# Layer norm with GELU on one core: the first row tile loaded in 32 and 96 partitions, the second from ScalarE's queue

## Chip, cores, metric

One core of a Trainium2 chip. The metric is device time in microseconds (us) of one execution. Before: 320.3 us, median of 6 runs (319.95 to 320.45). A profile's span is some 1.8 us shorter than the time of the same run.

## The reference

```python
x: (8, 1024, 2048) float32; gamma, beta: (2048,)
normalized = (x - mean(x, -1)) / sqrt(var(x, -1) + eps)
out = gamma * normalized + beta
return 0.5 * out * (1 + tanh(sqrt(2 / pi) * (out + 0.044715 * out ** 3)))
```

67.1 MB are read and 67.1 MB are written.

## The kernel before

The 8192 rows are 16 blocks of 4 MB, each of four row tiles (128 partitions x 2048). Five slots hold one block each; the result overwrites the input in its slot, is stored from there, and only then may the slot be loaded again.

```python
xg = xf.rearrange("(b p r) d -> b p r d", p=P, r=R)      # R = 4, SLOTS = 5, SPLIT = 3
# SyncE: all loads
for b in range(B):
    s = slot(b)
    if stored(b):
        sy.wait_ge(s_store[s], stored(b))
    for q in range(R):
        if b == 0:
            sy.dma_start(out=xts[s][:, q:q + 1], in_=xg[0, :, q:q + 1]).then_inc(s_first[q], 16)
        elif b == SPLIT:
            sy.dma_start(out=xts[s][:, q:q + 1], in_=xg[b, :, q:q + 1]).then_inc(s_load[s], 16)
    if b not in (0, SPLIT):
        sy.dma_start(out=xts[s], in_=xg[b]).then_inc(s_load[s], 16 * R)
# ScalarE: parameters, then arithmetic and stores
ac.preload_act_table(ACT.Gelu_apprx_tanh)
for k, (p, src) in enumerate(((64, gamma), (0, beta), (32, beta))):
    ac.dma_start(out=row(p), in_=src.rearrange("(o k f) -> o k f", o=1, k=K)).then_inc(s_par[k], 16)
... # [cut: beta to bf16, g_t from PSUM, then per tile yk = (x - mean) * rstd and the GELU; a store per block,
    #       in the last block one per tile]
# VectorE
for q in range(R):
    stats(slot(0), q, (s_first[q], 16), q + 1)
    ...  # [cut: after tile 0 it waits for g_t = gamma on all partitions, which eight matmuls make from gamma's row]
```

Of the kernel before, what the change touches and what calls it, by code (L numbers as in the profile page):

```python
# [10 lines left out]
R = 4  # L11
SLOTS = 5
SPLIT = 3
K = 16


@with_exitstack
def kernel(
# [9 lines left out]
    P = 128  # L28
# [9 lines left out]
    xg = xf.rearrange("(b p r) d -> b p r d", p=P, r=R)  # L38
# [8 lines left out]
    def sb(name, shape, dt):  # L47
        return pool.tile(shape, dt, name=name)

    xts = [sb(f"xt{s}", [P, R, d], f32) for s in range(SLOTS)]  # L50
    yks = [sb(f"yk{s}", [P, d], bf16) for s in range(2)]
    zgs = [sb(f"zg{s}", [P, d], bf16) for s in range(2)]
    pss = [psum.tile([P, d], f32, name=f"ps{s}") for s in range(2)]
    rows = sb("rows", [65, K, d // K + 4], f32)
    ones = sb("ones", [65, P], f32)
# [12 lines left out]
    def sem(name):  # L68
        return tc.alloc_semaphore(name)

    s_first = [sem(f"first{q}") for q in range(R)]
# [17 lines left out]
    def slot(b):  # L89
        return (b + SLOTS - 1) % SLOTS  # L90

    def row(p):
        return rows[p:p + 1, :, :d // K]

    def split(v):
        return v.rearrange("o (k f) -> o k f", k=K)

    def cols(j):
        return slice(j * FMAX, (j + 1) * FMAX)

    def by_row(b):
        return b == B - 1

    def stored(b):
        return sum(16 * (R if by_row(c) else 1) for c in range(b) if slot(c) == slot(b))

    with tc.tile_critical(no_gpsimd_drain=True):  # L107
        with nc.Block(no_gpsimd_drain=True) as block:

            @block.sync  # L110
            def _(sy):
                for b in range(B):
                    s = slot(b)
                    if stored(b):
                        sy.wait_ge(s_store[s], stored(b))
                    for q in range(R):
                        if b == 0:
                            sy.dma_start(out=xts[s][:, q:q + 1], in_=xg[0, :, q:q + 1]).then_inc(s_first[q], 16)
                        elif b == SPLIT:
                            sy.dma_start(out=xts[s][:, q:q + 1], in_=xg[b, :, q:q + 1]).then_inc(s_load[s], 16)  # L120
                    if b not in (0, SPLIT):
                        sy.dma_start(out=xts[s], in_=xg[b]).then_inc(s_load[s], 16 * R)
# [21 lines left out]
            @block.vector  # L144
            def _(ve):
                def stats(s, q, wait, count):
                    xr = xts[s][:, q].rearrange("p (s f) -> p s f", f=FMAX)
                    for j in range(nsub):
                        ins = ve.bn_stats(out=sts[:, q, j, :], in_=xr[:, j, :])  # L149
                        if j == 0 and wait:  # L150
                            ins._wait_ge(*wait)
                            if wait[0] is s_load[s]:
                                ins.then_inc(s_load[s], -16 * R)
                    ins.then_inc(s_o, 1)
                    ve.bn_aggr(out=mvs[:, q], in_=sts[:, q])._wait_ge(s_o, count).then_inc(s_a, 1)  # L155

                def scale(q, count):
                    ve.tensor_tensor(out=zgs[q % 2], in0=yks[q % 2], in1=g_t,  # L158
                                     op=ALU.mult)._wait_ge(s_n, count).then_inc(s_z, 1)

                ve.memset(b_hl, 0.0).then_inc(s_m, 1)  # L161
                for q in range(R):
                    stats(slot(0), q, (s_first[q], 16), q + 1)
                    if q == 0:

                        ve.tensor_tensor(out=split(b_hl[32:33]), in0=row(32), in1=split(b_hl[32:33]),  # L166
                                         op=ALU.subtract)._wait_ge(s_c, 2).then_inc(s_m, 1)
                        ve.wait_ge(s_c, 3)
                    else:
                        scale(q - 1, q)  # L170
                ve.sem_inc(s_o, -R)
                ve.sem_inc(s_n, -(R - 1))
                with ve.Fori(0, (B - 1) // SLOTS):
                    for k in range(SLOTS * R):
                        s, q = divmod(k, R)
                        stats(s, q, (s_load[s], 16 * R) if q == 0 else None, k + 1)
                        scale((q - 1) % R, k + 1)
                    ve.sem_inc(s_o, -SLOTS * R)
                    ve.sem_inc(s_n, -SLOTS * R)
                scale(R - 1, 1)  # L180

            @block.scalar
            def _(ac):
                ac.preload_act_table(ACT.Gelu_apprx_tanh)  # L184
                for k, (p, src) in enumerate(((64, gamma), (0, beta), (32, beta))):
                    ac.dma_start(out=row(p), in_=src.rearrange("(o k f) -> o k f", o=1, k=K)).then_inc(s_par[k], 16)
                ac.wait_ge(s_m, 1)
                ac.activation(out=split(b_hl[0:1]), in_=row(0), func=ACT.Identity)._wait_ge(s_par[1], 16).then_inc(s_c, 1)  # L188
                ac.activation(out=split(b_hl[32:33]), in_=row(32),  # L189
                              func=ACT.Identity)._wait_ge(s_par[2], 16).then_inc(s_c, 1)  # L190
                ac.activation(out=g_t, in_=pss[0], func=ACT.Identity)._wait_ge(s_tg, 1).then_inc(s_c, 1)  # L191
                for t in range(T + 1):
                    if t < T:
                        b, q = divmod(t, R)
                        ac.activation(out=yks[t % 2], in_=xts[slot(b)][:, q], func=ACT.Identity, scale=rss[:, q:q + 1],  # L195
                                      bias=nms[:, q:q + 1])._wait_ge(s_p, t + 1).then_inc(s_n, 1)
                    i = t - 1
                    if i < 0:
                        continue
                    b, q = divmod(i, R)  # L200
                    xt = xts[slot(b)]
                    ins = ac.activation(out=xt[:, q], in_=pss[i % 2], func=ACT.Gelu_apprx_tanh)._wait_ge(s_t, i + 1)  # L202
                    if by_row(b):
                        ins.then_inc(s_r, 1)
                        ac.dma_start(out=og[b, :, q:q + 1], in_=xt[:, q:q + 1])._wait_ge(  # L205
                            s_r, b + q + 1).then_inc(s_store[slot(b)], 16)
                        ac.sem_inc(s_g, 1)
                    elif q == R - 1:
                        ins.then_inc(s_r, 1)
                        ac.dma_start(out=og[b], in_=xt)._wait_ge(s_r, b + 1).then_inc(s_store[slot(b)], 16)  # L210
                        ac.sem_inc(s_g, 1)
                    else:
                        ins.then_inc(s_g, 1)

            @block.tensor
            def _(pe):

                pe.wait_ge(s_setp, 2)
                for j in range(nsub):
                    ins = pe.matmul(pss[0][:, cols(j)], lhsT=ones[64:65],  # L220
                                    rhs=rows[64:65, j * K // nsub:(j + 1) * K // nsub, :d // K], start=True, stop=True)
                    if j == 0:
# [60 lines left out]
```

## Time and profile before

| | before |
|---|---|
| time | 320.3 us |
| span of the profiled run | 318.5 us |
| bytes moved, at 430 GB/s | 134.24 MB, 312 us |
| gamma lands, g_t is ready | 6.02, 15.17 us |
| first store issued | 36.02 us |
| last load has landed for its user | 285.0 us |
| last store issued | 310.32 us |

The prediction shows the slices, the chain and the start. To read them: transfers are the bound from 3 us to 314 us (the DMA digit is 9 from the second slice to the last but one), so ask of every change what it does to the bytes moved by a given moment.

### The profile page before, as it was taken

Reading aid. Unit: us, or ns where it says so; the run is one execution under the profiler, and the core shown is the slowest. Engines: PE = TensorE matmul, PEld = TensorE weight load, DVE = VectorE, ACT = ScalarE, POOL = GpSimd, SP = SyncE. Lnnn points to the kernel's source line nnn. Section 1 sums busy time; section 2 is a strip of 40 time slices with the busy share of each in tenths; the row PEclk is TensorE's granted clock in tenths of the full one; section 3 lists DMA queues with packets and bytes.
Section 4 is the critical chain, followed back from the end, with each engine's and each line's share of the span. In section 5 each row is a group of like instructions: output and inputs, shape, how many; then the busy total and the mean of one; then the engine's idle time right before and its main releaser. Section 6 shows DMA issues by size and latency. Waiting matters only on the chain.

```text
span 318.5 us, 2090 instructions
## 1 busy us (share of the span) xinstructions
PE 244.3 (77%) x520; PEld 57.2 (18%) x520; DVE 247.5 (78%) x386; ACT 251.7 (79%) x132; POOL 110.6 (35%) x201
## 2 busy tenths in 40 slices
PE   2769999999999989687795868958589595886860
PEld 1212222222212112111121112212112121111110
DVE  3499999999999897786968968599686986869810
ACT  2769999999999989698696967969589695995970
POOL 1144444444444444232443333333332433324300
DMA  7999999999999999999999999999999999999995
GB/s 289 438 457 401 394 434 430 444 424 436 432 424 444 417 453 416 440 440 416 457 403 457 420 436 444 411 461 403 453 432 424 449 407 457 424 432 403 453 396 209
DMA packets 6002, 134.26 MB, mean 421 GB/s; under 512 B 704, under 2 KB 752, under 8 KB 752
## 3 DMA queue, kind: packets, MB, share of 16 engines
q1 hardware_dynamic: 3168, 67.11, 49.4%
q10 hardware_dynamic: 2832, 67.13, 49.0%
q14 instruction: 2, 0.02, 0.0%
HBM read 67.13 MB, written 67.11 MB: 421 GB/s over the span
## 4 chain that ended last, share of the span: by engine, by line
DMA 64%; ACT 14%; DVE 10%; POOL 5%; PE 3%; issue 1%; ACTq 0%; DVEq 0%; POOLq 0%; SPq 0%
DMA xt<-in_x_dram 32%; DMA out_dram<-xt 30%; ACT yk L195 9%; DVE sts L149 7%; ACT xt L202 4%; POOL ves L135 3%; DVE zg L158 2%; PE ps L220 2%; DMA rows<-in_gamma_dram 2%; POOL rss L137 2%; POOL nms L139 1%; DVE mvs L155 1%; PE ps L237 1%; ACT g_t L191 1%; ACTq L205 0%
## 5 line engine op out<-in xcount | busy, mean ns | idle before, releaser
L149 DVE BATCH_NORM_STATS2 sts<-xt 128x6 f32<-128x512 f32 x256 | 157.7, 679 | 33.5 <-DMA xt<-in_x_dram 31.9
L195 ACT ACTIVATE yk<-xt,nms,rss 128x2048 bf16<-128x2048 f32 x64 | 133.7, 2090 | 48.9 <-POOL nms L139 42.9
L237 PE MATMUL ps<-zg,ident 128*128 128x512 bf16 x256 | 120.8, 627 | 55.8 <-DVE zg L158 54.7
L233 PE MATMUL ps<-b_hl,ones_b 33*128 33x512 bf16 x256 | 120.6, 624 | 2.2 <-PEq L228 2.2
L202 ACT ACTIVATE xt<-ps 128x2048 f32<-128x2048 f32 x64 | 118.9, 1858 | 1.5 <-PE ps L237 1.5
L135 POOL TENSOR_SCALAR ves<-mvs 128x1 f32<-128x1 f32 x64 | 38.5, 602 | 179.2 <-DVE mvs L155 179.2
L158 DVE TENSOR_TENSOR zg<-yk,g_t 128x2048 bf16<-128x2048 bf16 x64 | 76.5, 1195 | 19.2 <-ACT yk L195 19.2
L237 PEld LDWEIGHTS ps<-zg,ident 128*128 128x128 bf16 x256 | 27.6, 130 | 149.0 <-DVE zg L158 113.7
L233 PEld LDWEIGHTS ps<-b_hl,ones_b 33*128 33x128 bf16 x256 | 27.0, 127 | 92.1 <-issue 88.4
L139 POOL TENSOR_SCALAR nms<-mvs,rss 128x1 f32<-128x1 f32 x64 | 35.7, 558 | 6.3
L137 POOL TENSOR_TENSOR rss<-ves,mhalf 128x1 f32<-128x1 f32 x64 | 35.3, 552 | 5.3
L155 DVE BATCH_NORM_AGGREGATE mvs<-sts 128x2 f32<-128x24 f32 x64 | 16.9, 264 | 2.2
L220 PE MATMUL ps<-rows,ones 1*128 1x512 f32 x8 | 7.2, 1076 | 6.1 <-DMA rows<-in_gamma_dram 6.1
L188 ACT ACTIVATE b_hl<-rows 1x2048 bf16<-1x2048 f32 x1 | 1.9, 1909 | 5.3 <-DMA rows<-in_beta_dram 5.3
L166 DVE TENSOR_TENSOR b_hl<-rows,b_hl 1x2048 bf16<-1x2048 f32 x1 | 2.3, 2280 | 2.8 <-ACT b_hl L189 2.8
L220 PEld LDWEIGHTS ps<-rows,ones 1*128 1x128 f32 x8 | 2.5, 327 | 9.2 <-DMA rows<-in_gamma_dram 6.1
L191 ACT ACTIVATE g_t<-ps 128x2048 bf16<-128x2048 f32 x1 | 1.9, 1877 | 1.9 <-PE ps L220 1.9
L184 ACT ACT_TABLE_LOAD x1 | 1.3, 1283 | 0.9 <-SPq L107 0.9
L189 ACT ACTIVATE b_hl<-rows 1x2048 bf16<-1x2048 f32 x1 | 1.9, 1908 | 0.0
L161 DVE MEMSET b_hl<- 33x1024 uint32 x1 | 0.9, 912 | 1.2 <-SPq L107 1.2
L126 POOL MEMSET ones<- 65x128 f32 x1 | 0.2, 202 | 0.5 <-SPq L107 0.5
L130 POOL TENSOR_SCALAR_AFFINE_SELECT ident<-ident 128x128 bf16<-128x128 bf16 x1 | 0.3, 295 | 0.1
(7 smaller groups left out, 0.9 us busy)
## 6 DMA issues: line engine op xcount, KB each, us to landing
out_dram<-xt ACTq DMA_DIRECT2D x15, 4096.0 KB, 32.6
xt<-in_x_dram SPq DMA_DIRECT2D x14, 4096.0 KB
xt<-in_x_dram SPq DMA_DIRECT2D x8, 1024.0 KB, 8.4
out_dram<-xt ACTq DMA_DIRECT2D x4, 1024.0 KB, 8.6
rows<-in_beta_dram ACTq DMA_DIRECT2D x2, 8.0 KB, 5.9
rows<-in_gamma_dram ACTq DMA_DIRECT2D x1, 8.0 KB, 5.1
```

Source lines behind the costliest of these rows:

```text
L135: po.tensor_scalar(out=ves[:, c], in0=mvs[:, k, 1:2], scalar1=float(eps), scalar2=1.0, op0=ALU.add, op1=ALU.mult)._wait_ge(s_a, k + 1).the ...
L137: po.tensor_tensor(out=rss[:, c], in0=ves[:, c], in1=mhalf, op=ALU.pow)._wait_ge(s_q, 2 * k + 1).then_inc(s_q, 1)
L139: po.tensor_scalar(out=nms[:, c], in0=mvs[:, k, 0:1], scalar1=rss[:, c], scalar2=-1.0, op0=ALU.mult, op1=ALU.mult)._wait_ge(s_q, 2 * k + 2 ...
L149: ins = ve.bn_stats(out=sts[:, q, j, :], in_=xr[:, j, :])
L155: ve.bn_aggr(out=mvs[:, q], in_=sts[:, q])._wait_ge(s_o, count).then_inc(s_a, 1)
L158: ve.tensor_tensor(out=zgs[q % 2], in0=yks[q % 2], in1=g_t, op=ALU.mult)._wait_ge(s_n, count).then_inc(s_z, 1)
L191: ac.activation(out=g_t, in_=pss[0], func=ACT.Identity)._wait_ge(s_tg, 1).then_inc(s_c, 1)
L195: ac.activation(out=yks[t % 2], in_=xts[slot(b)][:, q], func=ACT.Identity, scale=rss[:, q:q + 1], bias=nms[:, q:q + 1])._wait_ge(s_p, t + ...
L202: ins = ac.activation(out=xt[:, q], in_=pss[i % 2], func=ACT.Gelu_apprx_tanh)._wait_ge(s_t, i + 1)
L220: ins = pe.matmul(pss[0][:, cols(j)], lhsT=ones[64:65], rhs=rows[64:65, j * K // nsub:(j + 1) * K // nsub, :d // K], start=True, stop=True)
L233: ins = pe.matmul(ps[:, cols(j)], lhsT=ones_b, rhs=b_hl[:, cols(j)], start=True, stop=False)
L237: ins = pe.matmul(ps[:, cols(j)], lhsT=ident, rhs=zgs[k % 2][:, cols(j)], start=False, stop=True)
```

## The change

The intent is to start the stream of loads earlier: a small first load (32 partitions) should be issued faster, and a second queue should feed the engines from the start.

```diff
+FEW = 32
 ...
-                        if b == 0:
+                        if b == 0 and q == 0:
+                            for p in (slice(0, FEW), slice(FEW, P)):
+                                sy.dma_start(out=xts[s][p, q:q + 1], in_=xg[0, p, q:q + 1]).then_inc(s_first[q], 16)
+                        elif b == 0 and q != 1:
                             sy.dma_start(out=xts[s][:, q:q + 1], in_=xg[0, :, q:q + 1]).then_inc(s_first[q], 16)
 ...
-                    stats(slot(0), q, (s_first[q], 16), q + 1)
+                    stats(slot(0), q, (s_first[q], 32 if q == 0 else 16), q + 1)
 ...
             def _(ac):
+                ac.dma_start(out=xts[slot(0)][:, 1:2], in_=xg[0, :, 1:2]).then_inc(s_first[1], 16)
                 ac.preload_act_table(ACT.Gelu_apprx_tanh)
```

## The prediction

The sum: 320.22 - 0.5 + 0 = 319.7 us. In step 3, that tiles 0 and 1, 2 MB, pass ahead of gamma is the assumption.

> **What bounds the kernel now.** I read the 40 slices first, then the chain that ended last, then the first 20 us and the last 35 us in order of time with the bytes moved in each. The program has 64 tiles of 128 rows in 16 blocks of 4 MB; five buffers of one block each; loads on SyncE's queue, stores and the three parameter loads on ScalarE's.
>
> The slices: the DMA line is at 9 from the second to the last but one, while no compute engine is above 79% of the span.
>
> ```profile
> PE 244.3 (77%) x520; PEld 57.2 (18%) x520; DVE 247.5 (78%) x386; ACT 251.7 (79%) x132; POOL 110.6 (35%) x201
> DMA  7999999999999999999999999999999999999995
> GB/s 289 438 457 401 394 434 430 444 424 436 432 424 444 417 453 416 440 440 416 457 403 457 420 436 444 411 461 403 453 432 424 449 407 457 424 432 403 453 396 209
> HBM read 67.13 MB, written 67.11 MB: 421 GB/s over the span
> ```
>
> 134.24 MB have to pass. At the level of the middle slices (about 430 GB/s) that is 312 us; the span is 318.5. So some 6.5 us are not transfer at full rate: a start before the pipe is full, and an end. The change works on the start.
>
> The chain (start us, us, what): compute in the beginning, later store landing to load to landing, then the last block's arithmetic.
>
> ```profile
> 0.92 5.09 DMA rows<-in_gamma_dram
> 6.06 7.21 PE ps L220 x8
> 13.29 1.89 ACT g_t L191
> 15.27 2.48 DVE sts L149 x4
> ...
> 68.79 26.55 DMA out_dram<-xt
> 95.35 33.54 DMA xt<-in_x_dram
> ...
> 250.80 34.20 DMA xt<-in_x_dram
> ```
>
> It names gamma as the first link, since row tile 1 waits for the gamma product (15.27). This is where one can be misled: the chain follows who released whom, but the 26.55 and 33.54 us are transfers lying in a full queue. Store landings at 95.33 (block 2) and 250.79 (block 10) are 8 blocks apart: 19.43 us a block, 216 GB/s, half of 430. From the first store (issued at 36.0) stores and loads thus share the pipe in halves, and stores are never short of work: 36.0 + 0.34 + 3 x 19.43 = 94.6, against 95.33 seen. What sets the end is bytes over rate, plus when the pipe began to be full.
>
> The beginning, in stretches of 0.2 us (last columns DMA share and GB/s):
>
> ```profile
> 1.60:1.80 0.20, 0.00 (x0) 0.00 (x0) 0.20 (x1) 0.20 (x1) 0.20 (x1) 1.00 0.00 0
> 1.80:2.00 0.20, 0.00 (x0) 0.00 (x0) 0.20 (x1) 0.20 (x1) 0.02 (x1) 1.00 0.62 123
> 2.20:2.40 0.20, 0.00 (x0) 0.00 (x0) 0.00 (x0) 0.00 (x0) 0.00 (x0) 1.00 1.22 205
> 2.80:3.00 0.20, 0.00 (x0) 0.00 (x0) 0.00 (x0) 0.00 (x0) 0.00 (x0) 1.00 0.33 123
> 3.00:3.20 0.20, 0.00 (x0) 0.00 (x0) 0.00 (x0) 0.00 (x0) 0.00 (x0) 1.00 1.36 573
> ```
>
> SyncE begins its first load at 0.93; nothing moves before 1.8; from 1.8 to 3.0 it is some 170 GB/s, and full after 3.0. By 4.0 us 0.65 MB have moved, as much as a pipe at 430 GB/s would move in 1.51 us: the effective start is 4.0 - 1.51 = 2.5 us. That number is what the change can lower.
>
> [...] halves of 216 GB/s each when both queues are full. So no bandwidth is to be had here, only issue time. [...] here it is 0.87 us (0.93 to 1.80) for the 128-partition load, and its issue on SyncE took 0.775 us, the later ones of this line 0.376 to 0.43. [...]
>
> **The change part by part.**
>
> 1. Row tile 0 in 32 + 96 partitions. One issue more on SyncE (about 0.4 us by the later ones), and tile 1's is gone from it: the same count of four. [...] How much of its 0.775 us is a fixed cost the trace doesn't say; my estimate is that the first byte comes 0.1 to 0.4 us earlier, at 1.4 to 1.7.
>
> 2. Tile 1 on ScalarE's queue. It is issued there at 0.92, beside SyncE's first, not after it (before, SyncE's second load began near 1.7). From about 1.8 two queues feed the engines. The gap between 1.8 and 3.0, 0.2 MB moved where 0.52 would fit at 430, is worth (0.52 - 0.2)/0.43 = 0.7 us if filled entirely. But at 2.0 to 2.4 the share is already above 1 at only 205 to 246 GB/s, so a part is the first packets' own latency, which stays. I take a third to a half: 0.2 to 0.35 us.
> Sum of 1 and 2: effective start earlier by 0.3 to 0.75 us, the middle near 0.5.
>
> 3. Gamma and both betas behind tile 1 in the same queue. [...] 2 MB: 4.9 us at 430, so near 6.7 to 7 us; landing 1 to 2 us after that (tile 0's bytes were through near 5.0 and its consumer began at 5.86). Gamma then lands at 8 to 9 instead of 6.02: 2 to 3 us later. Tile 0, sharing the pipe with tile 1, lands near 7 to 7.5 instead of 5.83. Gamma is the later, and 7.2 us of matmuls and the 1.89 us copy follow it. So VectorE's second statistics start at 17.3 to 18.3 instead of 15.27, and all arithmetic and the first store (36.0) are 2 to 3 us later.
>
> 4. What this delay costs. While no store is there, loads take the whole pipe, so it isn't idle. Up to 36.3 some 0.43 x (36.3 - 2.5) = 14.5 MB are loaded of the 21 MB that five buffers admit; then 216 GB/s up to the first store's landing near 55.8 give 4.2 MB more, so about 2.3 MB of loads are in hand when the next is allowed. Three us of delay take 3 x 0.216 = 0.65 MB of these. They do not run out. Later VectorE waits for loads anyhow (31.9 us in 11 times), so arithmetic catches up. Cost at the end: 0.
>
> 5. The table preload starts some 0.6 us later behind the added issue; it was done at 2.17 and its first user starts after 7. Nothing.
>
> Last block: its load lands at 285.00, its last store is issued at 310.32 and lands 6.7 us later; a load alone took 4.9 with its start. So the arithmetic is about 1.8 us ahead of the queue at the end, and DMA is full up to 314. With stores beginning later and the pipe earlier, loads end sooner, and this margin grows. So the end follows the start of the pipe one to one. Sum: 320.22 - 0.5 + 0 = 319.7 us.
>
> **Rivals.**
> (a) The gamma delay reaches the end, as the chain would have it: +2 to +3, minus 0.5: 322 to 323 us. For it: gamma opens the chain, and the chain is arithmetic up to 68.8 us. Against: a full DMA line throughout that time, and 2.3 MB in hand. One in thirty.
> (b) The first packets' latency is all of the gap, and both queues' first issues are no faster: nothing gained, 320.0 to 320.4. For it: share over 1 at half the rate before 2.4. Against: 0.33 to 0.55 of share between 2.4 and 3.0, engines without work though a whole tile was queued. About one in four.
> (c) The gap is filled entirely and the first byte comes 0.4 us earlier: -1.1, 319.1 us. One in eight.
> (d) Other order of packets, other luck: dips such as 98 GB/s at 301 to 302 us, with stores queued, cost 0.8 us and may fall otherwise. Either way, +-0.4 us; this widens the range more than the start does.
> An exposed end is no serious rival, by the margin above.
>
> **Range and chances.** 319.7 from the sum; (b) and (c) with (d) give 319.0 to 320.5. For 2% it needs 6.4 us. The whole time outside full-rate transfer is 6.5 us, of which the change touches at most 1.1, so faster by 2% is out; slower needs more than (a). Within 2%: 97%.
>
> **What would show it.** In the changed trace: bytes before 1.8 us (step 1); more than the 0.65 MB by 4.0 us, near 0.8 to 0.95 (step 2); gamma's landing at 8 to 9 and the matmuls of the gamma product starting there, VectorE's second statistics at 17.3 to 18.3, first store at 38 to 39 (step 3); the DMA line at 9 through the 30 to 70 us, and the last load landing before 284 (step 4). It is wrong if DMA idles around 40 to 60 us, if bytes by 4.0 us are no more than before, or if the rate of the middle stretch changes.

## The result

321.94 us (median of 6, 321.78 to 322.03) against 320.3: ratio 1.0053, 95% interval 1.004 to 1.0066, so 0.5% slower, and within the 2% that count as the same. Ratios here are the mean time of one kernel's fast runs over that of the other's fast runs of the same rounds, not quite the ratio of the medians quoted. Spans 318.5 and 319.9 us, both at clock 1.0.

**Where the time went.** Stretches of the first 12 us, before (last columns DMA share and GB/s):

```profile
2.00:4.00 2.00, 0.00 (x0) 0.00 (x0) 0.12 (x1) 0.17 (x1) 0.00 (x0) 1.00 0.93 311
4.00:6.00 2.00, 0.00 (x0) 0.00 (x0) 0.14 (x1) 0.00 (x0) 0.00 (x0) 1.00 1.03 422
6.00:8.00 2.00, 1.94 (x3) 0.90 (x4) 2.00 (x4) 0.49 (x1) 0.00 (x0) 1.00 0.99 406
8.00:10.00 2.00, 2.00 (x4) 0.93 (x3) 0.59 (x2) 1.98 (x2) 1.02 (x3) 1.00 1.03 434
10.00:12.00 2.00, 2.00 (x3) 0.67 (x2) 0.61 (x1) 1.35 (x1) 0.00 (x0) 1.00 0.99 418
```

and after:

```profile
2.00:4.00 2.00, 0.00 (x0) 0.00 (x0) 0.12 (x1) 0.62 (x1) 0.00 (x0) 1.00 0.89 242
4.00:6.00 2.00, 0.00 (x0) 0.00 (x0) 0.00 (x0) 0.00 (x0) 0.00 (x0) 1.00 0.97 389
6.00:8.00 2.00, 0.00 (x0) 0.00 (x0) 0.00 (x0) 0.00 (x0) 0.00 (x0) 1.00 1.04 267
8.00:10.00 2.00, 0.91 (x1) 0.50 (x2) 0.00 (x0) 0.00 (x0) 0.00 (x0) 1.00 1.04 258
10.00:12.00 2.00, 2.00 (x4) 0.85 (x3) 1.33 (x3) 1.74 (x1) 0.00 (x0) 1.00 0.97 401
```

From 6 to 10 us the DMA share is as high as before, the rate is 262 instead of 420 GB/s: the engines are busy and slow. The queues in that stretch (packets, MB, share of 16 engines' time; q1 is SyncE's queue, q10 ScalarE's), before and after:

```profile
q1 hardware_dynamic: 223, 1.67, 99.7%
q10 hardware_dynamic: 43, 0.01, 1.1%
```

```profile
q1 hardware_dynamic: 138, 1.00, 96.9%
q10 hardware_dynamic: 115, 0.05, 7.0%
```

1.67 MB are 204 packets of 8 KB (the other packets are semaphore writes of 4 bytes); they took 0.997 x 16 x 4 us, 0.313 us each. After it is 1.00 MB, 122 packets, 0.51 us each. In this stretch SyncE's queue moves the 96 partitions of tile 0 (and, at its end, tile 2). Summed from the packets, the changed kernel is 0.25 us of transfer behind at 4 us, 0.4 at 6, 1.9 at 10 and 2.0 from 14 us on (differences of bytes over 430 GB/s). The first byte came no earlier: 1.8 to 2.0 us is the first stretch with bytes in both. The view puts a packet's bytes and its whole time into the stretch in which it begins, so the zero from 2.6 to 2.8 us says that no packet began there, not that the engines were idle:

```profile
1.80:2.00 0.20, 0.00 (x0) 0.00 (x0) 0.20 (x1) 0.20 (x1) 0.02 (x1) 1.00 2.24 287
2.40:2.60 0.20, 0.00 (x0) 0.00 (x0) 0.00 (x0) 0.20 (x1) 0.00 (x0) 1.00 0.10 41
2.60:2.80 0.20, 0.00 (x0) 0.00 (x0) 0.00 (x0) 0.02 (x1) 0.00 (x0) 1.00 0.00 0
```

0.8 us of the 2.0 come back at 38 to 41 us, early among the stores: there the kernel before moves 0.35 MB less than a full pipe while the changed one doesn't. Why, no run shows; the time of the first store alone does not decide it, since the cut in tile 3 below (first store at 36.05 us) does not lose it either. 1.2 us remain up to 280 us, and the end is 1.4 us later (span). The chain of the changed kernel (start us, us, what):

```profile
1.37 7.67 DMA rows<-in_gamma_dram
9.09 7.21 PE ps L225 x8
18.30 2.48 DVE sts L153 x4
...
71.77 25.98 DMA out_dram<-xt
97.77 31.25 DMA xt<-in_x_dram
...
253.41 31.77 DMA xt<-in_x_dram
285.26 2.48 DVE sts L153 x4
```

ScalarE in order of time has the first store:

```profile
39.04 0.36 ACTq L215 DMA_DIRECT2D out_dram<-xt  x1
```

Gamma lands 3.0 us later, the first store is issued 3.0 us later (39.04), yet the last load is used at 285.26, as before (285.10). A later first store leaves the whole pipe to the loads for longer, and that pays for the 2 us which the loads lost (without the cut, the same delay brings the last load forward by 1.9 us: "Tile 1's move alone" below). So the loads are level, and the stores, which share the same bytes, are late.

### The profile page after: what moved, and what is told of

It is laid out like the page before. It is cut to its first block, busy times and chain, and to the rows that moved or that the text cites. A ratio compares the mean times of both kernels' runs of the same rounds, so it can differ in the third digit from the quotient of the medians.

```text
span 319.9 us, 2091 instructions
## 1 busy us (share of the span) xinstructions
PE 244.3 (76%) x520; PEld 57.1 (18%) x520; DVE 247.4 (77%) x386; ACT 251.5 (79%) x132; POOL 112.4 (35%) x201
## 4 chain that ended last, share of the span: by engine, by line
DMA 63%; ACT 14%; DVE 10%; POOL 5%; PE 3%; issue 1%; ACTq 0%; DVEq 0%; POOLq 0%; SPq 0%
DMA out_dram<-xt 32%; DMA xt<-in_x_dram 29%; ACT yk L200 8%; DVE sts L153 7%; ACT xt L207 4%; POOL ves L139 3%; DMA rows<-in_gamma_dram 2%; DVE zg L162 2%; PE ps L225 2%; POOL rss L141 2%; POOL nms L143 1%; DVE mvs L159 1%; PE ps L242 1%; ACT g_t L196 1%; ACTq L210 0%
## 5 line engine op out<-in xcount | busy, mean ns | idle before, releaser
L143 POOL TENSOR_SCALAR nms<-mvs,rss 128x1 f32<-128x1 f32 x64 | 37.7, 589 | 6.3
L225 PEld LDWEIGHTS ps<-rows,ones 1*128 1x128 f32 x8 | 2.5, 326 | 12.2 <-DMA rows<-in_gamma_dram 9.1
```

The source lines that it names most:

```text
L143: po.tensor_scalar(out=nms[:, c], in0=mvs[:, k, 0:1], scalar1=rss[:, c], scalar2=-1.0, op0=ALU.mult, op1=ALU.mult)._wait_ge(s_q, 2 * k + 2 ...
L225: ins = pe.matmul(pss[0][:, cols(j)], lhsT=ones[64:65], rhs=rows[64:65, j * K // nsub:(j + 1) * K // nsub, :d // K], start=True, stop=True)
```

## The experiments

Theory P: the cut is the cost, because loads of 32 and of 96 partitions move slower than a whole tile at the same share of the engines' time (0.51 us for an 8 KB packet against 0.313, above). For each cut the author also expected a packet time and a loss. These rested on a picture of the hardware that no run here shows; the figures (such as 1.24 us lost, 0.62 us for a packet of a half) are guesses to be held against the measurement. Rival Q: the order of the queues, gamma behind tile 1.

Twelve kernels, all correct. They ran on three chips, each in rounds beside the kernel before on its own chip (319.8 to 320.7 us): the first four runs on one, the next four and the last two on another, the short and the long hole on a third. A run is called slow here by its time alone; the granted clock was 1.0 in all. "Lost" below is transfer behind the kernel before at 20 us, worked out from the packets as above.

### The cut alone

```diff
 # kernel before, SyncE, b == 0, q == 0; VectorE waits for 32
+for p in (slice(0, 32), slice(32, 128)):
+    sy.dma_start(out=xts[s][p, q:q + 1], in_=xg[0, p, q:q + 1]).then_inc(s_first[q], 16)
```

> The cut of row tile 0 into 32 + 96 partitions alone; tile 1 stays on SyncE's queue, parameters first on ScalarE's. Theory P [...]: 8 KB packets near 0.5 us instead of 0.31, a stretch of about 260 GB/s for some 3 us, 1.2 to 2 us of transfer lost by 14 us, time 1.2 to 2.2 us over before (321.5 to 322.5). Rival Q (the order of the queues: tile 1 ahead of gamma, arithmetic 3 us later): no cost here, 319.9 to 320.4.

329.26 us, but 322.29 to 331.47 in 6 runs: two fast (322.29, 326.31), four counted slow, over 1.5% above the fastest. The profiled one is the fastest. Lost: 1.5 us (1.2 to 2 expected); the rate of the 8 KB packets between 2 and 6 us is 252 GB/s (0.98 x 16 x 4 us for 122 packets, 0.51 us each). P holds for the start, Q falls. But the time is 2 us over before at the best and far more in most runs, which P's 1.5 us do not give.

### Tile 1's move alone

```diff
 # kernel before; SyncE leaves out tile 1
+ac.dma_start(out=xts[slot(0)][:, 1:2], in_=xg[0, :, 1:2]).then_inc(s_first[1], 16)
 ac.preload_act_table(ACT.Gelu_apprx_tanh)
```

> Tile 1 on ScalarE's queue ahead of the parameters, tile 0 whole. Theory P: no slow packets, rate full from about 3 us; gamma still 1.5 to 3 us late, first store near 38 to 39; no loss, and if the 0.7 to 0.8 us of transfer that before loses at 38 to 41 us is the first store meeting the 8 KB packets of block 3, the later store avoids it: 319.3 to 320.3. Rival Q: 1.5 us over before, 321.5 to 322.

320.62 us (320.49 to 320.9), ratio 1.0012 (0.9999 to 1.0025): the same, slightly above the range that P gave. Lost: 0.2 us. From 4 to 12 us the rate is 411 to 430 GB/s. Gamma lands at 9.2, the first store is issued at 39.17, the last load has landed at 283.1: the late gamma costs nothing, and it brings the loads forward. The gain hoped for at 38 to 41 us is there (0.8 us) but 1.3 us are lost elsewhere, at 60 to 80 us; why, I do not know.

### Halves

```diff
+for p in (slice(0, 64), slice(64, 128)):        # in place of 32 and 96
```

> Tile 0 cut into partitions 0 to 63 and 64 to 127, otherwise before. Theory P: [...] packets near 0.62 us, [...] 2.5 us more: time 2 to 2.7 us over before, and more than the 32 + 96 cut. Rival R ([...] the number of loads, make the cut slow): [...] one more load: equal to or below the 32 + 96 cut, under 1 us.

335.32 us (334.24 to 336.16), ratio 1.0468. Rates from 4 us on:

```profile
4.00:6.00 2.00, 0.00 (x0) 0.00 (x0) 0.00 (x0) 0.00 (x0) 0.00 (x0) 1.00 0.97 205
6.00:8.00 2.00, 1.61 (x2) 0.83 (x3) 0.00 (x0) 0.00 (x0) 0.00 (x0) 1.00 0.98 213
8.00:10.00 2.00, 2.00 (x4) 0.70 (x3) 1.52 (x3) 1.33 (x1) 0.00 (x0) 1.00 0.99 385
```

Half the rate of before (422 and 406 GB/s in the first two stretches) at a full share while the halves pass; from 4 to 8 us it is 100 packets of 8 KB in 0.94 x 16 x 4 us, 0.60 us each. Lost 2.6 us, 2.5 expected. Two equal parts lose more than 32 and 96, so rival R falls. The time, 15 us over before, is not P's again: P's range missed it by 12.

### The middle first

```diff
+for p in (slice(32, 96), slice(0, 32), slice(96, 128)):       # VectorE waits for 48
```

> Tile 0 cut into partitions 32 to 95, then 0 to 31, then 96 to 127. Theory P: the first, though 64 partitions like each half of the other cut, [...] its packets near 0.31 us; [...] 1.2 us lost, time 1 to 1.6 us over before, about half of what the halves lose. Rival R: three loads instead of two, at least as slow as the halves.

322.55 us (321.45 to 322.66). SyncE's queue while the 64 middle partitions pass (3.0 to 4.4 us), then while the two outer quarters pass (5 to 7 us):

```profile
q1 hardware_dynamic: 73, 0.49, 88.2%
```

```profile
q1 hardware_dynamic: 89, 0.49, 100.3%
```

0.49 MB are 60 packets of 8 KB: 0.33 us each in the middle, 0.53 us in the quarters. The middle has as many partitions as a half, whose packets took 0.60 us. Lost: 1.5 us (1.2 expected). The time is 2.3 us over before, more than the 1.6 I allowed, since here the last block sets the end (below). With that, P is as good as shown for the start: three cuts lose 1.5, 2.6 and 1.5 us, and a packet of 8 KB took 0.31 us in the whole tile, 0.33 in partitions 32 to 95, 0.51 with 32 + 96, 0.53 in the quarters and 0.60 in the halves. So the number of partitions alone does not set it, but which they are; why, no run shows.

### The same cut in a full pipe

```diff
 # kernel before; the 32 + 96 cut at q == 3 in place of q == 0
```

> The same 32 + 96 cut, but of row tile 3, whose load lies in a full pipe and which nobody waits for until 24 us; queues and parameters as before. Theory P [...]: [...] 1.24 us of transfer lost between 10 and 16 us, the 96-partition packets near 0.5 us; gamma and first store as before (36.0). Last load near 287.5, last block still behind the queue: time 1.0 to 1.6 us over before (321.2 to 322). Rival S (the cut costs only at the very start, by late first bytes and a late first tile): within 0.3 us of before.

329.53 us, 324.69 to 335.77; three fast runs (324.7 to 325.6), three slow. The queue between 10 and 14 us, 0.54 us for each 8 KB:

```profile
q1 hardware_dynamic: 155, 1.05, 108.8%
```

Lost 2.2 us, more than the 1.24 expected: the packets that follow are slow too (the 32 KB packets begun between 14 and 16 us took 1.5 us in the mean instead of 1.21). Rival S falls: it is not a matter of the first bytes. Again the time lies beyond what the loss explains.

### The changed kernel with the parameters first

```diff
 # changed kernel, ScalarE: tile 1's load after the three parameter loads
```

> The changed kernel with gamma and beta in front of tile 1 on ScalarE's queue. Theory T (the late first store pays back: stores that begin later leave the loads more of the pipe, so the last load lands earlier; the price of the cut is the queue's 1.2 to 2 us or, where the store begins early, a last block that ends after the queue): gamma 3 to 4 us earlier than in the changed kernel, first store near 35, last load near 289 instead of 285.3, end set by the last block's 25 us of arithmetic: no better than the changed kernel, 321.8 to 324 (up to 331 if the slow runs of the cut alone come again). Rival Q (gamma behind tile 1 is the cost): back to 320.3 or below.

334.67 us (331.91 to 334.87). Gamma lands at 4.5, the first store is issued at 34.64, and the kernel is 13 us slower than with gamma late. Q falls altogether: with the cut there, the late gamma helps the changed kernel, it does not cost. My number was wrong too: the last load is not at 289 but at 298.5 us.

### The cut by columns

```diff
-for p in (slice(0, FEW), slice(FEW, P)):
-    sy.dma_start(out=xts[s][p, q:q + 1], in_=xg[0, p, q:q + 1]).then_inc(s_first[q], 16)
+for f in (slice(0, FMAX), slice(FMAX, d)):
+    sy.dma_start(out=xts[s][:, 0, f], in_=xg[0, :, 0, f]).then_inc(s_first[q], 16)
```

> The changed kernel with tile 0 cut by columns (512 + 1536 of 2048) instead of by partitions, so both loads reach all 128 partitions [...]; tile 1 and the parameters as in the changed kernel. Theory P: no slow packets, rate full from about 3 us, like tile 1 alone on ScalarE's queue: 320.2 to 320.9. Rival (the count of loads or their order at the start is the cost): as the changed kernel, 321.5 to 322.2.

320.29 us (five of six between 320.02 and 320.41, one 323.62), before 320.24. The changed kernel with the cut along the other axis: same number of loads, same order, all 128 partitions in each, no loss of rate (406 to 425 GB/s from 4 to 12 us). So the changed kernel's 1.6 us are the partition cut.

### Halves with the move

```diff
 # changed kernel; (slice(0, 64), slice(64, P))
```

> The changed kernel with tile 0 cut into 0 to 63 and 64 to 127. [...] 2.5 us lost, 3 with the stall seen in the changed kernel. The open part is the other 12 us of the halves without the move. If they come from the early first store (a last load that is too late), the late gamma takes them away: 322.2 to 323.5. If the halves themselves leave one DMA engine falling behind for the whole kernel, they stay: 332 to 336.

321.94 us (321.86 to 322.48). Lost 2.4 us, and yet 13 us faster than the halves alone. So the halves as such do not make the kernel slow for good; what was with them does.

### What is it, then? Holes without a cut

Two things make up the excess. First the end. In nine runs the span is the last load's landing plus 31.5 to 32 us: 289.0 and 320.5 for the cut alone, 289.2 and 320.7 for the middle cut, 300.9 and 332.5 for the halves. This is the last block's four tiles of arithmetic and one short store, and nothing is left to hide it. In the kernel before it is 33.5, in the changed one 34.7: there the queue of stores is the later, with 2 to 3 us to spare. Delayed loads with an early first store eat up that spare time.

Second, the middle. Per 100 us (150 to 250 us) most kernels move 43.3 MB, but some 42.3 to 42.8, their packets of 32 KB taking up to 2.3 us. I noticed that these are those in which the stores trail the loads by a certain distance, and tried it with a wait in place of any cut:

```diff
 # kernel before, SyncE, b == 0
+if q == 2:
+    sy.wait_ge(s_first[1], 16)     # short hole;  s_c, 1: long hole;  s_par[1], 16: the smallest
```

> The kernel before without any cut, but SyncE waits until tile 1 has landed before it issues tile 2: a hole of about 1.7 us in the loads from 7.4 us on, gamma and first store as before. Theory D (the excess of the cuts over their 1.2 to 2.5 us comes from how far the stores trail the loads: at 80 us 14.0 MB before, 14.4 to 15.0 in all steady runs, but 13.1 to 13.4 in the four whose packets are slow [...]; 12.65 in the middle cut, steady again): distance 14.0 - 1.7 x 0.43 = 13.3 MB, so slow packets, a growing spread of the engines, and 324 to 336 us with scatter, without any partition cut. Rival C (the cut by partitions itself leaves the engines out of step): packets at 1.213 us as before, time 320.2 + 1.7, at most 322.5, with little scatter.

> The same with a longer hole: SyncE waits for the first beta copy to be done (9.4 us), so tile 2's bytes begin near 10.3, a hole of about 2.9 us. Theory D: distance 14.0 - 1.25 = 12.75 MB, beyond the slow band, so packets steady and the time less than with the shorter hole: last load near 285 + 2 x 2.9 = 290.8, last block 30 us after that, 321 to 323.5. Rival C: about 2.9 us over before too (323), so this run alone tells little; the two together do: D has the longer hole faster by 2 us or more, C slower by about 1. Rival M (anything that brings the loads later makes the whole kernel slow): 330 or more.

323.85 us (323.33 to 324.87) and 325.14 us (324.75 to 326.53). Lost 2.6 and 3.2 us; the distances came to 12.6 and 11.9 MB, so the short hole jumped over the band that it was meant to hit, and D's order (the longer hole faster) did not come. Both are steady, with the end set by the last block: 290.5 + 31.6 = 322.1 and 293.2 + 31.5 = 324.7. This confirms the end, not the band. The long hole's time also missed my 321 to 323.5, since I took its last load 2.4 us too early.

> The shorter hole came out at 2.6 us (release to first byte took 1.8 us, not 1.0) and put the distance at 12.56 MB, below the slow band, so it did not try theory D. Here SyncE waits only for the first beta copy's landing (7.2 to 7.5 us), so the hole should be 1.8 to 2.1 us and the distance 12.9 to 13.4 MB. Theory D: slow packets and engines falling behind without any partition cut, 324.5 to 336 with scatter; slower than the longer hole's 323.85. Rival C (the partition cut itself does it): steady packets, last load near 289, 322 to 323.2, faster than the longer hole.

The 1.8 us in this expectation are misread: in the short hole tile 1's last packet ended at 8.11 us and tile 2's first began at 9.65, which is 1.5 us.

Lost only 0.6 us (the hole was smaller than meant), distance 13.5 MB: 333.88 us, with two fast runs (324.79, 325.43) and four slow ones of 333.8 to 335.6. Even its fast runs (mean 325.1, ratio 1.0152, 1.0135 to 1.017) are slower than the hole that loses 2.6 us (mean 324.0, ratio 1.0117, 1.0095 to 1.0139), though they lost 2 us less at the start. The two intervals just overlap and the runs were on different chips, so the times alone are thin; the packets say more. What the two queues moved between 150 and 250 us, for this kernel and for the hole of 2.6 us:

```profile
DMA packets 1461, 42.40 MB, mean 424 GB/s; under 512 B 167, under 2 KB 167, under 8 KB 167
```

```profile
DMA packets 1509, 43.29 MB, mean 433 GB/s; under 512 B 188, under 2 KB 188, under 8 KB 188
```

No partition is cut here, so rival C falls. This is the one run of those aimed at the band that came near it.

```diff
 # the halves, with the short hole
```

> The cut into halves (335.3 us) with the hole of 2.6 us added: about 5 us of transfer lost by 16 us, distance 11.5 to 12.2 MB. Theory D: out of the slow band, packets steady, end set by the last block, 326 to 329: less time than the halves alone, with 2.6 us more lost. Rival C: 335 or more, as the cut is still there.

327.03 us: four fast runs of 325.73 to 327.23, two slow of 338 and 340. Its profile (fast) is steady, 43.3 MB in those 100 us. Lost 4.9 us, and its fast runs are some 9 us faster than the halves (335.3) that lose 2.6. The distance was 11.2 MB at 60 us, 10.1 at 70 and then 13.8 at 80, not the 11.5 to 12.2 I expected; it left the band upwards. Its two slow runs have no trace.

All fourteen together (fast profiled runs; distance: loads less stores moved by 80 us; rate: MB moved from 150 to 250 us; both summed from the packets):

| kernel | lost, us | first store, us | distance, MB | rate, MB | last load landed, us | span, us |
|---|---|---|---|---|---|---|
| before | 0 | 36.0 | 14.0 | 43.3 | 285.0 | 318.5 |
| changed | 2.0 | 39.0 | 14.7 | 43.3 | 285.2 | 319.9 |
| move alone | 0.2 | 39.2 | 14.9 | 43.3 | 283.1 | 318.6 |
| columns | 0.2 | 37.3 | 15.0 | 43.3 | 282.4 | 318.4 |
| halves + move | 2.4 | 38.2 | 14.4 | 43.3 | 285.9 | 320.6 |
| halves + hole | 4.9 | 36.7 | 13.8 | 43.3 | 293.5 | 325.0 |
| smallest hole | 0.6 | 35.9 | 13.5 | 42.4 | 291.8 | 323.6 |
| cut in tile 3 | 2.2 | 36.0 | 13.4 | 42.4 | 291.9 | 323.8 |
| parameters first | 1.4 | 34.6 | 13.4 | 42.6 | 298.5 | 330.0 |
| halves | 2.6 | 36.3 | 13.2 | 42.3 | 300.9 | 332.5 |
| cut alone | 1.5 | 34.6 | 13.1 | 42.8 | 289.0 | 320.5 |
| middle | 1.5 | 34.0 | 12.7 | 43.3 | 289.2 | 320.7 |
| short hole | 2.6 | 36.0 | 12.6 | 43.3 | 290.5 | 322.1 |
| long hole | 3.2 | 35.9 | 11.9 | 43.3 | 293.2 | 324.7 |

The five with a lower rate are those from 13.1 to 13.5 MB, and no other. One moment is a crude measure (before swings between 13.4 and 14.1 MB within a block), but the mean from 80 to 200 us parts them too: 13.05 to 13.37 MB in the five, 12.76 and 13.69 in the nearest others. The band was read off the first ten kernels as 13.1 to 13.4 MB and is stretched here to 13.5 for the one run that came near it since. So within this kernel the distance is a sign of the slow packets, not a cause shown. Why a distance of reads and writes should slow the packets, and why parts of a load then end late (the ends of the last block's load lay 14 us apart in the halves, 3.6 before), no run here shows. That stays open.

## Why the prediction was wrong, point by point

- **What bounds the kernel** (bytes over rate, plus the start): right for both kernels. Neither has its end set by the last block (33.5 and 34.7 us after the last load's landing, where 31.5 is the floor).
- **What the cut costs**: this is the step that failed. The prediction set no term at all for it. Each of the two loads does end in sixteen semaphore writes in the trace, like a whole tile, and the engines' share is as high, but a packet takes 0.51 us instead of 0.313. Measured on the cut alone, the term is 1.5 us of transfer lost; with the move beside it, 2.0; sign and size of the sum follow from this (+1.6 us instead of -0.5). The columns show the rest of the change to be worth nothing either way.
- **Step 1, first byte 0.1 to 0.4 us earlier**: wrong, and from a misreading. The 0.775 us are the longest of the four issues, the fourth, which began at 2.30 us. The first whole tile was issued as fast as the 32 partitions are after (SyncE's queue, before, then after), so the issue had nothing to save:

```profile
0.93 0.38 SPq L118 DMA_DIRECT2D xt<-in_x_dram  x1
```

```profile
0.93 0.38 SPq L120 DMA_DIRECT2D xt<-in_x_dram  x1
```

  In the changed kernel the first byte came in the same stretch, 1.8 to 2.0 us, so in both 0.87 to 1.07 us after the issue at 0.93. The cut alone had 0.25 MB by 3 us against 0.17, worth under 0.2 us, and lost it at once.
- **Step 2, the gap filled by a second queue**: wrong. 0.54 MB by 4.0 us instead of 0.65 (one of the prediction's own signs of being wrong), and with tile 0 whole still 0.52 against 0.58 before, when a packet's bytes are spread over its time. There was no gap: the shares of 0.33 to 0.55 that the prediction took for engines without work count a packet's time where it begins. Spread over their time, the packets of before keep 0.90 to 1.00 of the engines busy from 2.4 to 3.0 us; the first sixteen took 0.71 us each, the later ones 0.31. Of the rivals (b), the first packets' latency is all of the gap, was right in this part.
- **Step 3, the delay**: gamma at 8 to 9 was 9.04, second statistics at 17.3 to 18.3 were 18.30, first store at 38 to 39 was 39.04. The sizes were right at their upper edge. The order was not: tile 0's 96 partitions did not share the pipe evenly with tile 1; between 3 and 6 us ScalarE's queue moved 0.95 MB and SyncE's 0.16. SyncE's first 32 packets had begun by 3.5 us, its 33rd began at 5.8, when tile 1 was nearly through. Tile 0 landed at 10.6 us, not 7 to 7.5. With tile 0 whole (the move alone) tile 1 was not through first: between 6 and 10 us SyncE's queue moved 1.25 MB and ScalarE's still 0.41. What decides it, no run shows.
- **Step 4, the delay costs nothing**: right, and shown by the move alone (gamma 3 us later, 1.0012). More than that: the delay gives the loads time alone, and with gamma early the same cut took 334.67 us.
- **"this margin grows"**: it did, by 1.2 us (33.5 to 34.7), but not because the loads ended sooner: the last one landed at 285.2, not before 284, since the loss at the start took back what the delay gave. The prediction's own sums had both terms, with the start a gain instead of a loss.
- **Rival (a)**, the gamma delay reaching the end, gave 322 to 323, close to the time measured. The number fits by chance: the reason is another.

## What to carry to other kernels

When a load is cut into parts of the partitions, measure the packet time of each part: here a full share of the engines went with half the rate (205 to 213 GB/s in the halves), the cut along the free axis kept the rate (406 to 425 GB/s), and of the ranges of partitions only 32 to 95 came near it (0.33 us for 8 KB against 0.31). In a kernel bound by transfers, work out how late the last load may land (here 31.5 us before the end) and what the first store's time does to it; in this kernel an earlier first store came with a later end (34.64 us and 334.67 against 39.04 and 321.94). And look at the packets' mean time in the middle of the run before believing that a small delay at the start costs only itself.
